# Other step orders in a two-layer hybrid network: the recurrence, the attention, half-array products without mutual order, and the last tile's low part in a bank of its own

## The chip, the cores and the metric

The kernel runs on one core of one Trainium2 chip. The metric is the device time of one execution in microseconds (us), lower being better. The engines are TensorE (PE in the profile, its weight loads PEld), VectorE (DVE), ScalarE (ACT), GpSimd (POOL) and SyncE (SP), which here issues nearly all transfers.

## The reference, cut to what matters

Two layers run over 256 tokens of width 1024. Layer 0 mixes tokens by a gated linear recurrence (HGRN2, 8 heads of 128), layer 1 by sparse attention (NSA, 16 query heads, 4 key heads, three branches: compressed, selected and windowed). A SwiGLU network of hidden width 2816 follows each mixer.

```
for layer in range(2):
    h = modulate(x, norm_mix[layer], shift, scale)
    y = hgrn2_mixer(h, ...) if layer == 0 else nsa_mixer(h, ..., nsa_shared_kv(...))
    x = x + gate * y
    h = modulate(x, norm_ffn[layer], shift, scale)
    x = x + gate * ((silu(h @ w_a) * (h @ w_b)) @ w_out)
```

Shift, scale and gate come from a vector c by one matrix for each sublayer (the ada products). All is float32.

## The kernel before

**Precision.** Each weight tile is split into a high part wh (ScalarE casts it to f32r, L321) and a low part wl (VectorE subtracts, L325); activations are split likewise. A product is the sum of three f32r products, wh by high, wh by low, wl by high (mm3, L531 to L533; tok_steps, L983 to L985, with the operands' roles exchanged), each over 128x128 weights and 256 columns. Where high and low activations lie side by side, the first two are one product of 512 columns (gemm_wide, L543), and wl by high is one of 256 (L544). Products of 32 or 64 weight columns (level_scores, ada_pe, head_norm, attend_values) are in plain fp32; they use a part of the array's columns, four or two of them side by side.

**Order of the work.** A weight tile of 1 MB is loaded by SyncE in the order of SCHED through a ring of 4, cast and split when its turn comes (process, fetch). ORDER["hgrn"] and ORDER["nsa"] are lists written by hand; they set in which order the program's steps are written, and SCHED follows from them. The framework's scheduler then lists the instructions of each engine by priority (PRI, high_priority) and by the dependencies known to it; an engine takes its list in order.

**The recurrence (hgrn).** In its list D builds the decays of a pair of head pairs, i and g are weight products (values hg_i, gates hg_g), S the scores of a pair (hgrn_scores: psl for levels 0 to 4 and psu for level 5, in the 32-column form, psx for the last level), V the products of scores and values (hgrn_values: hgpv, L1134 to L1136, fp32 on the whole array, waiting for the masked scores A), T the normalised values' transposes (values_end: hgt), o the output product (hgo). A step with + is not written at its place: it is a generator put into the row `between`, and hgrn_scores takes steps from it, 4 after each of its 12 blocks of a level in S0/4 and S1/4. The token x writes whatever is left.

**The attention (nsa).** In its list c is half of the compression (cmp), q a query product (nq0 to nq3, its copies huq and hsqq and the rotation usq, QR on ScalarE and VectorE), K the normalised input for keys and values, G the gates product, n the norm of two queries (hs, hb), w a product for values (tiles v0 and v1 of the profile), x the compressed branch (cs, its softmax css on VectorE and ScalarE, its transpose pct), s the scores of one pair of heads (L1521, maxima mx and exponentials Pt, normalised at L1547), v the values of one pair (transposes ptt at L1561, copies PT at L1564 and L1566, products po at L1578) and a one tile of the ada products (L427: adapsg, adapsss, with the transpose adat). attend_values is listed late (offset 10 of "av"), rotate early (offset -15 of "rot").

**The end.** In the second SwiGLU network each of the eight output tiles of 128 columns is 22 steps of gemm_wide into the two halves of one PSUM bank, and residual (L796) adds first the low half, then the high half, to x; for the last network it then writes the tile to memory (L800).

## Time and profile before

| what | value |
|---|---|
| median of 3 runs (lowest, highest) | 726.69 us (726.45, 727.84) |
| the profiled execution | 726.5 us |
| its span | 724.7 us |
| TensorE busy | 711.4 us, 98% |
| VectorE busy | 578.6 us, 80% |
| ScalarE busy | 433.7 us, 60% |
| recurrence, first psl to first hgo product | 70.7 to 146.7 us |
| attention, first hs to first nso product | 384.3 to 508.5 us |

The profile is of one execution, taken by the hardware. The span is what its records cover; 1.8 us of the execution's time lie around it. A row of the timeline has the start in us, the duration, the engine, the line and the operation with output and inputs; "x4" counts records, and an fp32 product has two. A duration of TensorE includes the pipeline's run, so what one product takes of its time is read from start to start. The view of waits names the engine and line that waited and what it waited for, with the sum, the times and the longest in us.

### The profile page before, as it was taken

How to read it: one execution, taken by the hardware profiler on the slowest of the kernel's cores; microseconds unless marked ns; L12 is line 12 of the kernel's file. 1: busy time of each engine (PE TensorE's matmuls, PEld its weight loads, DVE VectorE, ACT ScalarE, POOL GpSimd, SP SyncE). 2: the span in 40 equal slices, each digit the busy share in tenths (PEclk: the TensorE clock that was granted, in tenths of full speed). 3: DMA queues.
4: the chain of work that ended last, by engine and by line, in shares of the span. 5: the costliest groups of instructions: out<-in, count | busy, mean ns of one | idle time of the engine just before them, and what ended most of it. 6: DMA issues, size and time to landing. Idle time of an engine off the chain costs nothing.

```text
span 724.7 us, 14519 instructions
## 1 busy us (share of the span) xinstructions
PE 711.4 (98%) x5821; PEld 626.3 (86%) x5821; DVE 578.6 (80%) x1177; ACT 433.7 (60%) x849; POOL 0.4 (0%) x5
## 2 busy tenths in 40 slices
PE   7999999999999999999998999999999999999997
PEld 4998788799999999988897996555999888888886
DVE  6997896589999889889598898677779878776651
ACT  5669877567635454544379776558657656564430
POOL 0000000000000000000000000000000000000000
PEclk9999999999999999999999999999999999999999
DMA  8899865734599889889546631663745757556710
GB/s 354 323 395 359 338 249 187 282 117 175 176 335 378 318 334 345 317 307 339 194 147 232 232 124 52 233 233 123 284 175 175 250 207 256 205 196 231 256 65 23
DMA packets 27158, 172.48 MB, mean 238 GB/s; under 512 B 2897, under 2 KB 4305, under 8 KB 7250
## 3 DMA queue, kind: packets, MB, share of 16 engines
q1 hardware_dynamic: 26656, 170.80, 64.2%
q8 instruction: 46, 0.75, 0.4%
q10 hardware_dynamic: 434, 0.74, 0.3%
q14 instruction: 22, 0.18, 0.1%
HBM read 170.48 MB, written 1.05 MB: 237 GB/s over the span
## 4 chain that ended last, share of the span: by engine, by line
PE 84%; ACT 7%; DVE 6%; DMA 2%; issue 1%; ACTq 0%
PE ffo L543 11%; PE ff L531 6%; PE ff L533 6%; PE ff L532 6%; PE ffo L544 6%; PE ff L543 5%; PE po L1578 3%; PE ff L544 2%; PE adapsss L427 2%; PE ptt L1561 2%; PE s L1521 1%; PE nso L531 1%; ACT wh L321 1%; PE nso L533 1%; PE cmp L1416 1%; PE hg_g L531 1%
## 5 line engine op out<-in xcount | busy, mean ns | idle before, releaser
L321 ACT CAST wh<-raw 128x1024 fp32r<-128x1024 f32 x199 | 206.7, 1048 | 152.2 <-PE ffo L543 47.7
L325 DVE TENSOR_TENSOR wl<-raw,wh 128x1024 fp32r<-128x1024 f32 x199 | 241.3, 1222 | 64.7 <-ACT wh L321 64.4
L543 PE MATMUL ffo<-g,wh 128*128 128x512 f32 x352 | 123.6, 394 | 0.0
L532 PE MATMUL ff<-hl,wh 128*128 128x256 f32 (+1 forms) x352 | 99.2, 282 | 0.0
L544 PE MATMUL ffo<-g,wl 128*128 128x256 f32 x352 | 99.1, 282 | 0.0
L533 PE MATMUL ff<-hh,wl 128*128 128x256 f32 (+1 forms) x352 | 99.1, 282 | 0.0
L531 PE MATMUL ff<-hh,wh 128*128 128x256 f32 (+1 forms) x352 | 99.0, 282 | 0.0
L543 PEld LDWEIGHTS ffo<-g,wh 128*128 128x128 f32 x352 | 66.2, 188 | 15.5
L389 DVE CUSTOM_DVE_ANT_0 junk<-raw,crep 128x1024 f32<-128x1024 f32 x64 | 78.0, 1218 | 0.5 <-DMA raw<-in_w 0.4
L531 PEld LDWEIGHTS ff<-hh,wh 128*128 128x128 f32 x352 | 66.3, 189 | 0.2 <-ACT hh L582 0.2
L533 PEld LDWEIGHTS ff<-hh,wl 128*128 128x128 f32 x352 | 66.5, 189 | 0.0
L532 PEld LDWEIGHTS ff<-hl,wh 128*128 128x128 f32 x352 | 66.4, 189 | 0.0
L544 PEld LDWEIGHTS ffo<-g,wl 128*128 128x128 f32 x352 | 66.1, 188 | 0.0
L543 PE MATMUL ff<-h,wh 128*128 128x512 f32 x152 | 54.1, 394 | 0.0
L544 PE MATMUL ff<-h,wl 128*128 128x256 f32 x152 | 42.6, 281 | 0.0
L543 PEld LDWEIGHTS ff<-h,wh 128*128 128x128 f32 x152 | 28.7, 189 | 6.6
L465 ACT ACTIVATE Pt<-Pt,nm 128x128 f32<-128x128 f32 x64 | 28.2, 443 | 8.5 <-DVE nm L1530 8.4
L796 DVE SCALAR_TENSOR_TENSOR x<-ffo,mod,x 128x256 f32<-128x256 f32 x32 | 15.4, 482 | 20.0 <-PE ffo L544 19.7
L544 PEld LDWEIGHTS ff<-h,wl 128*128 128x128 f32 x152 | 28.7, 189 | 0.0
L526 ACT CAST g<-fg 128x256 fp32r<-128x256 f32 x44 | 17.8, 404 | 17.8 <-DVE fg L1201 16.7
L1526 DVE CUSTOM_DVE_ANT_0 Pt<-s,cst 128x128 f32<-128x128 f32 (+1 forms) x64 | 19.1, 352 | 2.8 <-PE s L1521 2.8
L1037 DVE TENSOR_TENSOR rf<-rf 128x512 f32<-128x512 f32 x28 | 18.5, 692 | 2.2 <-ACT X L1034 1.2
(490 smaller groups left out, 1733.2 us busy)
## 6 DMA issues: line engine op xcount, KB each, us to landing
raw<-in_w SPq DMA_DIRECT2D x153, 1024.0 KB, 5.1
raw<-in_w SPq DMA_DIRECT2D x11, 512.0 KB, 6.6
w1late<-in_w SPq DMA_DIRECT2D x2, 1024.0 KB, 6.1
x<-in_x SPq DMA_DIRECT2D x2, 512.0 KB, 4.9
out<-x SPq DMA_DIRECT2D x8, 128.0 KB, 1.9
cst<-in_cst ACTq DMA_DIRECT2D x1, 558.0 KB
rselr<-in_rsel SPq DMA_DIRECT2D x1, 256.0 KB, 3.7
w<-in_w SPq DMA_DIRECT2D x1, 128.0 KB, 3.6
```

What stands on the lines that cost most here:

```text
L321: r = nc.scalar.copy(wh, u)
L325: r = nc.vector.tensor_tensor(wl, u, wh.bitcast(F32), op=ALU.subtract)
L389: r = nc.vector.tensor_tensor_reduce(out=junk, in0=t[:, h * D:(h + 1) * D], in1=self.crep, scale=1.0, scalar=0.0, op0=ALU.mult, op1=ALU.ad ...
L465: r = nc.scalar.activation(out, in_, func, **kw)
L531: mm(ps, lhsT=wh, rhs=hh, start=first, stop=False)
L532: mm(ps, lhsT=wh, rhs=hl, start=False, stop=False)
L533: return mm(ps, lhsT=wl, rhs=hh, start=False, stop=last)
L543: mm(ps, lhsT=w[k][0], rhs=b, start=k == 0, stop=False)
L544: mm(ps[:, 0], lhsT=w[k][1], rhs=b[:, 0], start=False, stop=k == n - 1)
L1037: nc.vector.tensor_tensor(fr, fr, ap(rf, 2 * W, [1, 2], [2, n], [0, b]), op=ALU.mult)
L1526: nc.vector.tensor_tensor_reduce(out=Pt[half][:, br, o:o + n], in0=ps[half][:, br], in1=cs[:, S - n:], scale=1.0, scalar=-3e38, op0=ALU.ad ...
L1578: nc.tensor.matmul(po[64 * half:64 * half + 64, t], lhsT=w[:, half], rhs=rhs, start=n == 0, stop=n == len(steps) - 1, tile_position=(0, 64 ...
```

## The change

There are four edits.

1. ada_pe (L427) and attend_values (L1578) declare no dependency between products that write other partitions of the same PSUM tile. No instruction is added; the scheduler may list them in another order.
2. In the recurrence, V0 moves behind D1, i2 and i3's place, and +g3 behind S1/4. S1 has 48 places for steps; i3 (16), g2 (16) and T0 (2) fill 34 of them, and g3 is written unbroken by x.
3. In the attention the compression and the gates come before nq0, nq2 before the values' products and the first norm, nq3 after both values' products, and the ada steps earlier among the last pairs. SCHED, and with it the order of the weight tiles, follows.
4. The last output tile puts its 22 low products into a bank of its own (ffo1_low), adds them to x, and then takes 44 products of 256 columns (wh and wl by the high part) into the other bank, whose one residual step is followed by the output.

The assert writes no instruction. The diff:

```diff
 
 ORDER = {
     "hgrn": (
-        "D0 k i0 +g0 +i1 +g1 S0/4 x c0 c1 V0 D1 i2 +i3 +g2 +T0 +g3 S1/4 x G0 V1 T1 o0 H o1 G1 o2 o3"
+        "D0 k i0 +g0 +i1 +g1 S0/4 x c0 c1 D1 i2 +i3 V0 +g2 +T0 S1/4 +g3 x G0 V1 T1 o0 H o1 G1 o2 o3"
     ).split(),
     "hada": [1, 1, 2, 2, 3, 3, 4, 4, 7, 7, 8, 8],
     "f0": [7, 7, 8, 8, 9, 13, 15, 16, 16, 16, 21, 21, 22, 23, 25, 26, 28, 29, 31, 32],
     "nsa": (
-        "q0 c1 c0 K G q1 n0 x0 w0 s0 q3 s1 q2 w1 s2 v0 v1 n1 s3 a s4 v2 a v3 a x1 s5 a a s6 v4 v6 s7 v5 a v7 a a a a a a"
+        "c1 c0 G q0 K q1 q2 n0 x0 w0 s0 s1 w1 q3 s2 v0 v1 n1 s3 a s4 v2 a v3 a a x1 s5 a s6 a v4 v6 s7 a a v5 a v7 a a a"
     ).split(),
     "f1": [15, 16, 24, 29],
 }
@@ -423,10 +423,13 @@
         ks = [i] if ss else [2 * i, 2 * i + 1]
         last = i == (7 if ss else 3)
         for n, k in enumerate(ks):
+            row = []
             for j in range(4):
-                nc.tensor.matmul(self.aps[32 * j:32 * j + 32, :q], lhsT=self.c32[:, k],
-                                 rhs=t[:, n * D + j * q:n * D + (j + 1) * q], start=k == 0, stop=k == KD - 1,
-                                 tile_position=(0, 32 * j))
+                row.append(nc.tensor.matmul(self.aps[32 * j:32 * j + 32, :q], lhsT=self.c32[:, k],
+                                            rhs=t[:, n * D + j * q:n * D + (j + 1) * q], start=k == 0, stop=k == KD - 1,
+                                            tile_position=(0, 32 * j)))
+                for r in row[:-1]:
+                    self.tc.declare_no_dep(row[-1].ins, r.ins, query=mybir.DependencyQuery.ANY, reason="other partitions")
         if not last:
             return
         m, A, bias = self.ada_tiles(l)
@@ -965,6 +968,7 @@
                 elif t[0] == "o":
                     for _ in out_steps(n):
                         pass
+            assert next(between, None) is None
             self.end_residual(nxt)
             self.h = nxt
 
@@ -1216,8 +1220,19 @@
                             tiles[nch * 16 + 8 * h + e] = t
                     nch += 1
                 ps = self.acc_tile(f"ffo{l}_{m}")
-                self.gemm_wide(ps, [tiles.pop(m * NF + k) for k in range(NF)], lambda k: g[:, k])
-                self.residual(ps[:, 0], m, gate, nxt, ps[:, 1])
+                ws = [tiles.pop(m * NF + k) for k in range(NF)]
+                if nxt is None and m == KD - 1:
+                    mm, pl = nc.tensor.matmul, self.acc_tile(f"ffo{l}_low")
+                    for k in range(NF):
+                        mm(pl[:, 0], lhsT=ws[k][0], rhs=gl[:, k], start=k == 0, stop=k == NF - 1)
+                    self.residual(pl[:, 0], m, gate, nxt, part=True)
+                    for k in range(NF):
+                        for e in range(2):
+                            mm(ps[:, 0], lhsT=ws[k][e], rhs=gh[:, k], start=k == 0 and not e, stop=k == NF - 1 and e == 1)
+                    self.residual(ps[:, 0], m, gate, nxt)
+                else:
+                    self.gemm_wide(ps, ws, lambda k: g[:, k])
+                    self.residual(ps[:, 0], m, gate, nxt, ps[:, 1])
             self.end_residual(nxt)
             self.h = nxt
 
@@ -1572,11 +1587,16 @@
             for e, t in ((0, slice(0, S)), (1, slice(P, S))):
                 steps.append((br, self.V[:, e, br, P * g:P * g + P].rearrange("p (h d) -> p h d", h=2),
                               slice(0, S) if e == 0 else slice(S, 384), t))
+        done = [], []
         for n, (br, w, r, t) in enumerate(steps):
             for half in range(2):
                 rhs = r if br is None else PT[half, br][:, r]
-                nc.tensor.matmul(po[64 * half:64 * half + 64, t], lhsT=w[:, half], rhs=rhs, start=n == 0,
-                                 stop=n == len(steps) - 1, tile_position=(0, 64 * half))
+                done[half].append(nc.tensor.matmul(po[64 * half:64 * half + 64, t], lhsT=w[:, half], rhs=rhs, start=n == 0,
+                                                   stop=n == len(steps) - 1, tile_position=(0, 64 * half)))
+        for a in done[0]:
+            for b in done[1]:
+                self.tc.declare_no_dep(b.ins, a.ins, query=mybir.DependencyQuery.ANY, reason="other partitions")
+                self.tc.declare_no_dep(a.ins, b.ins, query=mybir.DependencyQuery.ANY, reason="other partitions")
         self.split(self.O[0][:, j, :256], self.O[1][:, j, :256], po)
```

On TensorE, where the first values' products (hgpv) stand in the recurrence; in the names the last number counts buffers, hg_i2 is a values' product of f32r, hgpv0 and hgpv1 are those of the first two head pairs. Before:

```order
L1134 MATMUL hgpv0_1388<-v0_755,A0_1366 128x128
L1135 MATMUL hgpv0_1388<-v0_755,A0_1366 128x128
L1136 MATMUL hgpv0_1388<-v0_755,A0_1366 128x128
L983 MATMUL hg_i2_1493<-wh28_0_1245,h0_181 128x256
L984 MATMUL hg_i2_1493<-wl28_0_1246,h0_181 128x256
L1134 MATMUL hgpv1_1400<-v0_755,A1_1379 128x128
L1135 MATMUL hgpv1_1400<-v0_755,A1_1379 128x128
L1136 MATMUL hgpv1_1400<-v0_755,A1_1379 128x128
```

After:

```order
L988 MATMUL hg_i2_1460<-wl28_1_1250,h0_181 128x256
L989 MATMUL hg_i2_1460<-wh28_1_1249,h0_181 128x256
L1138 MATMUL hgpv0_1521<-v0_755,A0_1366 128x128
L1139 MATMUL hgpv0_1521<-v0_755,A0_1366 128x128
L1140 MATMUL hgpv0_1521<-v0_755,A0_1366 128x128
L1138 MATMUL hgpv0_1521<-v0_755,A0_1366 128x128
L1139 MATMUL hgpv0_1521<-v0_755,A0_1366 128x128
L1140 MATMUL hgpv0_1521<-v0_755,A0_1366 128x128
L1138 MATMUL hgpv1_1533<-v0_755,A1_1379 128x128
```

Before, hg_i2 is broken into by hgpv0 and by hgpv1; now all 48 of its products stand ahead of both.

On TensorE, at the end of the second scores; psu2 and psu3 are of the 32-column form, hg_g3 is a gates product of f32r. Before:

```order
L532 MATMUL hg_g3_1883<-h0_181,wh33_1_1712 128x256
L533 MATMUL hg_g3_1883<-h0_181,wl33_1_1713 128x256
L1114 MATMUL psu3_1919<-s1_758 32x64 x2
L1118 MATMUL psu3_1919<-X3_5_1483 32x32 x2
L1114 MATMUL psu3_1919<-s1_758 32x64 x2
L1118 MATMUL psu3_1919<-X3_5_1483 32x32 x2
L1114 MATMUL psu3_1919<-s1_758 32x64 x2
L1118 MATMUL psu3_1919<-X3_5_1483 32x32 x2
L1114 MATMUL psu3_1919<-s1_758 32x64 x2
L1118 MATMUL psu3_1919<-X3_5_1483 32x32 x2
L531 MATMUL hg_g3_1883<-h0_181,wh33_1_1712 128x256
```

After:

```order
L1122 MATMUL psu2_1864<-X2_5_1446 32x32 x2
L1118 MATMUL psu3_1865<-s1_758 32x64 x2
L1122 MATMUL psu3_1865<-X3_5_1450 32x32 x2
L1118 MATMUL psu3_1865<-s1_758 32x64 x2
L1122 MATMUL psu3_1865<-X3_5_1450 32x32 x2
L1118 MATMUL psu3_1865<-s1_758 32x64 x2
L1122 MATMUL psu3_1865<-X3_5_1450 32x32 x2
L1118 MATMUL psu3_1865<-s1_758 32x64 x2
L1122 MATMUL psu3_1865<-X3_5_1450 32x32 x2
L428 MATMUL adapsss1_1097<-raw34_1580,c32_103 32x512 x3
L428 MATMUL adapsss1_1097<-raw35_1699,c32_103 32x512 x4
L534 MATMUL hg_g3_1964<-h0_181,wh33_0_1708 128x256
```

Before, psu2 and psu3 each stand between products of hg_g3; now psu3 follows psu2, ada products of the same form follow, and hg_g3 comes behind them.

On ScalarE, in the attention, after the last exponentials of pair 1 (Pt1): V copies a values' product, huq3, hsqq3 and usq3 belong to query product nq3, hry is the norm's first step, PT0 are copies of pair 0's transposes, Pt2 the exponentials of pair 2. Before:

```order
L465 ACTIVATE Pt1_5585,sm_5584<-Pt1_5585,nm_5602 128x256
L1339 COPY V_4660<-v1_5690 128x2x256
L465 ACTIVATE hry_5867<-hs_5862,eps_88 128x256
L1566 COPY PT0_10_5793<-ptt_5794 128x384
L1566 COPY PT0_01_5799<-ptt_5800 128x384
L465 ACTIVATE Pt2_5752,sm_5751<-Pt2_5752,nm_5769 128x128
```

After:

```order
L468 ACTIVATE Pt1_5585,sm_5584<-Pt1_5585,nm_5602 128x256
L1243 COPY huq3_5738<-nq3_5689 128x512
L1245 ACTIVATE hsqq3_5740<-nq3_5689 128x512
L1255 COPY usq3_5742<-huq3_5738 32x512 x4
L468 ACTIVATE hry_5867<-hs_5862,eps_88 128x256
L1581 COPY PT0_10_5793<-ptt_5794 128x384
L1581 COPY PT0_01_5799<-ptt_5800 128x384
L468 ACTIVATE Pt2_5752,sm_5751<-Pt2_5752,nm_5769 128x128
```

Where one copy of v1 stood between the exponentials of pair 1 and hry, there stand now the three steps on nq3.

## The prediction

> **What bounds the kernel now.** I read the page first: busy shares, slices, granted clock, the chain.
>
> ```profile
> span 724.7 us, 14519 instructions
> PE 711.4 (98%) x5821; PEld 626.3 (86%) x5821; DVE 578.6 (80%) x1177; ACT 433.7 (60%) x849; POOL 0.4 (0%) x5
> PE   7999999999999999999998999999999999999997
> PEclk9999999999999999999999999999999999999999
> PE 84%; ACT 7%; DVE 6%; DMA 2%; issue 1%; ACTq 0%
> L796 DVE SCALAR_TENSOR_TENSOR x<-ffo,mod,x 128x256 f32<-128x256 f32 x32 | 15.4, 482 | 20.0 <-PE ffo L544 19.7
> ```
>
> TensorE is busy 98% of the span at full clock in every slice, and 84% of the chain that ended last is its work. So time goes only if TensorE does less, stands still less, or if something leaves the few us after its last product. The change leaves the amount of arithmetic as it was. What remains are three things: waits of TensorE, the price of changing the form in which its array is used, and the tail. The waits of TensorE come second:
>
> ```profile
> PE hs L1255 <- ACT hsqk L1305: 1.0, 1, 1.0
> PE nq L531 <- ACT wh L321: 1.0, 1, 1.0
> PE s L1521 <- DVE mx L1526: 0.7, 2, 0.4
> ```
>
> All three lie in the attention stage, 2.7 us together. No wait of the recurrence is in this view at such a size; what is to be won there are changes of form.
>
> **The recurrence.** The timeline of TensorE shows one visit of the 32-column form (psl, fp32) between full-array f32r products (hg_i, L983 to L985):
>
> ```profile
> 117.89 0.27 PE L985 MATMUL hg_i<-wh,h 128*128 128x256 f32 x1
> 118.10 0.45 PE L1108 MATMUL psl<-X 128*32 128x16 f32 x32
> 118.47 0.39 PE L983 MATMUL hg_i<-wh,h 128*128 128x256 f32 x1
> 118.70 0.28 PE L984 MATMUL hg_i<-wl,h 128*128 128x256 f32 x1
> 118.82 0.28 PE L985 MATMUL hg_i<-wh,h 128*128 128x256 f32 x1
> ```
>
> Start to start an f32r product of 256 columns takes 0.12 us (118.70 to 118.82). Into psl it takes 0.21, so entering costs 0.09. The first f32r product after it takes 0.23, 0.11 too much; I add 0.09 for leaving the form, an estimate set equal to the entry. Coming back is thus 0.20, a round trip 0.29. Between f32r and fp32 products that both use the whole array it is cheaper:
>
> ```profile
> 103.80 0.28 PE L985 MATMUL hg_i<-wh,h 128*128 128x256 f32 x1
> 104.15 0.49 PE L1135 MATMUL hgpv<-v,A 128*128 128x128 f32 x2
> 105.14 0.39 PE L1136 MATMUL hgpv<-v,A 128*128 128x128 f32 x2
> 105.29 0.37 PE L983 MATMUL hg_i<-wh,h 128*128 128x256 f32 x1
> 105.49 0.28 PE L984 MATMUL hg_i<-wl,h 128*128 128x256 f32 x1
> ```
>
> The first product after hgpv takes 0.20 (105.29 to 105.49), 0.08 too much, and the way in some 0.07: 0.15 a round trip. From 103.80 to 104.15 there are 0.35 us where 0.12 and 0.07 are due: a wait of 0.16 for the masks A.
>
> I count the changes of form in the listed order between the first psl and the first hgo product: 65 before, 54 after. Of these, f32r to 32 columns go from 23 to 19 (4 x 0.09 = 0.36), the way back from 24 to 21 (3 x 0.20 = 0.60), f32r to whole-array fp32 and back from 14 to 9 (2.5 x 0.15 = 0.38), and one change between fp32 forms is added (0.09). That is -1.25. The wait for A goes too, since 48 products of hg_i2 (5.7 us) now stand ahead of hgpv: -0.15. Sum -1.4.
>
> What it may cost: the values' normalisation chain starts about 5 us later against the score blocks. hgt0 and hgt1 need o0 and o1, and in the new order only six f32r products stand between the last adaps product and adat, which needs ScalarE's copy. Before, hgt1's place already shows a short wait:
>
> ```profile
> 130.80 1.90 PE L427 MATMUL adapsss<-raw,c 128*32 128x512 f32 x10
> 132.78 0.65 PE L1163 MATMUL hgt<-cst,o 128*128 128x128 f32 x4
> ```
>
> In the 1.98 us up to the second hgt stand a group of four column products and one torn from the next group; at the 1.06 us that a group's row has they fill it, without its pipelined end (some 0.9 each) 0.2 is a wait. If two such waits are added and the changes of form are worth only their cheap 0.07 each, the recurrence brings 11 x 0.07 - 0.4 = 0.4; if each is worth the dear 0.20 and no wait comes, 11 x 0.20 + 0.15 = 2.3. I take 1.4, since each part has its own row.
>
> **No ordering between half-array products.** TensorE takes its list in order, so the edit acts only through the list. Halves side by side run together; a torn pair does not:
>
> ```profile
> 449.67 1.08 PE L1578 MATMUL po<-PC,VC 128*64 128x256 f32 x4
> 454.39 1.30 PE L1578 MATMUL po<-PT,V 128*64 128x256 f32 x10
> ```
>
> Four records of one half (two products) need 1.08 us; ten of paired halves 1.30. An unpaired product of 256 columns is thus worth about 0.45. In the new list po's products form as many short groups as before and need one 256-column slot less (-0.45); hs, a column-tiled product without the edit, is torn once more (+0.45). Net 0, bounds -0.9 and +0.9.
>
> **The attention order.** By the same count, entries into f32r go from 18 to 15 (3 x 0.20), exits from 17 to 14 (3 x 0.09), changes between fp32 forms from 49 to 51 (2 x 0.09): -0.7. The waits of s for mx fall where VectorE put a rotation between the row maxima:
>
> ```profile
> 439.63 0.75 DVE L1244 SCALAR_TENSOR_TENSOR usq<-usq,cols,cst 128x512 f32<-128x512 f32 x1
> ```
>
> Now nq2's rotation is finished before s0: I take -0.5 of the 0.7. The other two waits of 1.0 (hs for hsqk, nq for a weight cast) keep their producers and nearly the queue ahead of these, so I leave them; they are worth 1.0 each if they went.
>
> Against this stand two new waits. First, pct follows the softmax chain of the compressed branch:
>
> ```profile
> 429.35 1.42 PE L1485 MATMUL cs<-KC,QN 128*128 128x32 f32 x12
> 436.15 0.42 DVE L1501 TENSOR_TENSOR css<-css,cmx 128x256 f32<-128x256 f32 x1
> 436.86 0.38 PE L1504 MATMUL pct<-cst,css 128*128 128x128 f32 x2
> ```
>
> The chain ran from 430.8 to 436.6, 5.8 us, with three rotation steps of about 0.7 on VectorE among its own, and TensorE filled the gap with 52 f32r products. Now 35 stand there, 35 x 0.12 = 4.2 us. If all three rotation steps are gone from it the chain takes 3.7 and nothing waits; if none is, 1.6 us are waited. I take a chain of 4.7, halfway, as subtractions of weights may stand in their place: +0.5.
>
> Second, nq3 takes v1's place as the filler between the scores of pairs 1 and 2 (21 products, 2.5 us, instead of 39, 4.6 us), and it is followed on ScalarE by three steps, not one. ScalarE's rows there:
>
> ```profile
> 436.48 0.60 ACT L1230 ACTIVATE hsqq<-nq 128x512 f32<-128x512 f32 x1
> 437.09 2.50 ACT L1240 COPY usq<-huq 32x512 f32<-32x512 f32 x4
> 441.39 0.40 ACT L465 ACTIVATE Pt<-Pt,nm 128x128 f32<-128x128 f32 x1 [1.80 <-DVE nm L1530]
> 448.43 0.58 ACT L1339 COPY V<-v 128x512 f32<-128x512 f32 x1
> 451.39 0.47 ACT L465 ACTIVATE hry<-hs,eps 128x256 f32<-128x256 f32 x1 [2.38 <-PE hs L1255]
> ```
>
> After the exponentials (441.39 to 448.4) came one copy of 0.58 and 2.38 of idle time, 2.96. Now huq, hsqq and usq of nq3 stand there: 0.6 + 0.6 + 2.5 = 3.7. Behind them are queued hry and the copies PT of the transposed probabilities, and behind those the exponentials of pair 2, on which ptt waits. So ScalarE delivers 0.7 us later while TensorE, with 18 fillers less, asks 2.1 us earlier: 2.8 less slack. How much there was is bounded by the idle 2.38 and by the ada products (adapsg) that stand ahead of the later ptt; I take +0.7, with 0 and +2.8 as ends. Sum of the attention: -0.7 - 0.5 + 0.5 + 0.7 = 0.0; ends -1.2 and +3.2.
>
> **The tail.** The last tile's timeline:
>
> ```profile
> 720.19 0.28 PE L544 MATMUL ffo<-g,wl 128*128 128x256 f32 x1
> 720.31 0.39 PE L543 MATMUL ffo<-g,wh 128*128 128x512 f32 x1
> 720.32 0.19 PEld L544 LDWEIGHTS ffo<-g,wl 128*128 128x128 f32 x1
> 720.54 0.28 PE L544 MATMUL ffo<-g,wl 128*128 128x256 f32 x1
> 720.86 1.00 DVE L796 SCALAR_TENSOR_TENSOR x<-ffo,mod,x 128x256 f32<-128x256 f32 x2 [6.67 <-PE ffo L544]
> 721.89 0.33 SPq L800 DMA_DIRECT2D out<-x  x1
> ```
>
> A wide pair takes 0.35 (720.19 to 720.54), 22 pairs 7.7 us; three products of 256 columns at 0.12 take 0.36, as much. Two residual steps (L796, 482 ns each) stood behind the last product; one is now done under the 44 products of the high part. -0.5, because nothing else stands between product and output.
>
> The new split has 22 weight loads more, one for each 256 columns instead of one for 512. The page counts as many loads as products (PEld and PE, 5821 each), so hg_i's products above have one each, and follow at 0.12 us all the same. [...]
>
> **Sum.** -1.4 (recurrence) + 0 (halves) + 0.0 (attention) - 0.5 (tail) = -1.9. The profiled execution took 726.5, 724.7 of it span and 1.8 around it; the median of the runs is 726.69. So 726.69 - 1.9 = 724.8.
>
> **The rivals.** *A, the attention order gives the gain back* (0.17). ScalarE's longer queue costs 2.0 instead of 0.7 and pct 0.8: the attention is at +1.6, the sum at -0.3, 726.4. For it: 2.8 us of slack are taken; against it: 2.38 of idle time were there.
>
> *B, slower* (0.11). The one mechanism is ScalarE's queue between pair 1 and pair 2: when hry and PT come late, pair 2's exponentials and, one after the other, the pairs behind it come late, so that the wait is paid at two pairs. It decides from 4.1 us at this place on (0.7 and the 3.4 up to 728.14); with 4.2 the time is 728.3. For it: each pair's 3.5 us of exponentials (16 of them from 441.39 to 448.4 for two pairs) stand in one queue. Against it: the ada products moved between the pairs are there to fill.
>
> *C, the attention gains as well* (0.14): neither new wait shows and one of the two waits of 1.0 goes with the moved weights: -1.2 - 1.0 in the attention, 722.6.
>
> *D, weight loads show in the tail* (0.03): were each of the 22 new loads to stand between two products with its profiled 0.19, the tail would be 4.2 longer and the time 729.0. [...] The stream of hg_i, with a load for each product, speaks against it.
>
> *That the change does nothing* can't be for the tail; for the freed halves it is my forecast.
>
> **How the numbers follow.** The forecast holds 0.55, with its own range of 723.6 to 726.0. A measurement of this kernel tells about 0.2% from no change, 1.45 us: faster is below 725.24, slower above 728.14. Of the 0.55 I count 0.40 as faster, 0.15 as same; C adds 0.14 to faster, A 0.17 to same, B 0.11 and D 0.03 to slower: 0.54, 0.32, 0.14. The range of 722.6 to 727.5 takes in A and C and leaves B out.
>
> **What would show it.** The stretch from the first psl product to the first hgo product should be about 1.4 us shorter, with hgpv unbroken behind hg_i2 and psu2, psu3 in one piece. The wait of s for mx should be gone; new rows should name pct behind css, and ptt or po behind ScalarE's PT. At the end one L796-like step of 0.5 us should stand between the last product and the output. The prediction is wrong if the recurrence gains under 0.5, if TensorE waits over 3 us more in the attention, or if the last tile's products take over 8.5 us.

## The result and the profile after

The changed kernel took 722.24 us (median of 6 runs, 721.75 to 723.39), the kernel before beside it 726.57 (6 runs, 726.22 to 727.84): a ratio of 0.9939, 95% interval 0.9926 to 0.9952, which is 4.4 us less (3.5 to 5.4). The forecast was 1.9 less, and 724.8 with a range down to 722.6: the sign was right, the size under half, and the time lies just outside the range. The profiled execution took 721.75. From the page of the changed kernel, the span, the busy shares, the granted clock's slices, and the chain's shares:

```profile
span 720.0 us, 14569 instructions
PE 708.3 (98%) x5843; PEld 626.2 (87%) x5843; DVE 579.6 (80%) x1177; ACT 433.4 (60%) x849; POOL 0.4 (0%) x5
PEclk9999999999999999999999999999999999999999
PE 88%; ACT 6%; DVE 4%; issue 1%; DMA 1%; SPq 0%; ACTq 0%
```

TensorE is still the bound, at full clock (98% busy, a mean granted clock of 1.00); the other engines have the same work. To find where the time went I cut each span at five starts on TensorE: the first psl, hgo, hs, the second network's first ff, and the last product. Those of the changed kernel, by its timeline:

```profile
69.81 0.55 PE L1112 MATMUL psl<-q,X 128*32 128x48 f32 x32
144.20 0.36 PE L534 MATMUL hgo<-oh,wh 128*128 128x256 f32 x1
381.67 0.62 PE L1270 MATMUL hs<-hsqk,cst 128*32 128x256 f32 x4
526.38 0.28 PE L534 MATMUL ff<-hh,wh 128*128 128x258 f32 x1
716.30 0.28 PE L1231 MATMUL ffo<-g,wl 128*128 128x256 f32 x1
```

With the same starts of the trace of before (70.65, 146.71, 384.26, 530.68, 720.54):

| stretch | before | after | difference | forecast |
|---|---|---|---|---|
| start to first psl | 70.65 | 69.81 | -0.84 | none |
| recurrence, to first hgo | 76.06 | 74.39 | -1.67 | -1.4 |
| rest of layer 0, to first hs | 237.55 | 237.47 | -0.08 | 0 |
| attention, to first ff | 146.42 | 144.71 | -1.71 | 0.0 |
| second network, to the last product | 189.86 | 189.92 | +0.06 | 0 |
| behind the last product | 4.16 | 3.70 | -0.46 | -0.5 |
| span | 724.7 | 720.0 | -4.70 | -1.9 |

The first row isn't the change's: two kernels below whose first 70 us are those of before reach psl at 69.96 (the attention's order alone) and 70.44 (the tail alone). Without it the change is worth 3.9 us, inside the measured interval. The second row has a scatter too: the profiled executions with the old list of the recurrence take 75.88 to 76.41 for it, those with the new one 74.39 to 74.90, 1.5 less by their medians. The attention is the term that was missed. The windows of these two stretches give the length, TensorE's busy time and the granted clock, before and after:

```profile
384.26:530.68 146.42, 143.31 (x1101) 1.00 0.52 193
```

```profile
381.67:526.38 144.71, 142.00 (x1102) 1.00 0.51 190
```

TensorE is busy 1.31 us less and stands still 0.40 less (3.11 to 2.71). At an equal clock I put that down to the list: fewer changes of form, or fewer torn groups (products on different columns of the array run side by side as a group: in a run below eight records of one take 1.07 us, and two alone 1.05; a group is torn when other products stand between its members). And the waits, forecast to grow by 0.7, have shrunk. The view of waits of the changed kernel, the rows of the attention:

```profile
PE nq L534 <- ACT wh L321: 0.8, 1, 0.8
PE po L1594 <- DVE mx L1541: 0.7, 1, 0.7
PE adat L441 <- ACT adasm L438: 0.5, 1, 0.5
PE hs L1270 <- ACT hsqk L1320: 0.5, 1, 0.5
PE ptt L1576 <- DVE Pt L1562: 0.2, 1, 0.2
```

The row of s behind mx is gone, as forecast. pct and the copies PT, for which 0.5 and 0.7 were put in, have no row. po waits, but for VectorE's maxima; adat's wait is new; and hs waits half as long as before.

### The profile page after: what moved, and what is told of

Its sections match the earlier page's. It is cut to its first block, busy times and chain, and to the rows that moved or that the text cites. A ratio compares the mean times of both kernels' runs of the same rounds, so it can differ in the third digit from the quotient of the medians.

```text
span 720.0 us, 14569 instructions
## 1 busy us (share of the span) xinstructions
PE 708.3 (98%) x5843; PEld 626.2 (87%) x5843; DVE 579.6 (80%) x1177; ACT 433.4 (60%) x849; POOL 0.4 (0%) x5
## 3 DMA queue, kind: packets, MB, share of 16 engines
HBM read 170.48 MB, written 1.05 MB: 238 GB/s over the span
## 4 chain that ended last, share of the span: by engine, by line
PE 88%; ACT 6%; DVE 4%; issue 1%; DMA 1%; SPq 0%; ACTq 0%
PE ffo L546 11%; PE ff L534 7%; PE ff L536 7%; PE ff L535 6%; PE ffo L547 5%; PE ff L546 5%; PE po L1594 2%; PE ff L547 2%; PE adapsss L428 2%; PE ptt L1576 2%; PE s L1536 2%; PE hg_g L534 1%; PE nso L534 1%; PE hgo L534 1%; PE hg_g L536 1%; PE nso L536 1%
## 5 line engine op out<-in xcount | busy, mean ns | idle before, releaser
L546 PE MATMUL ffo<-g,wh 128*128 128x512 f32 x330 | 116.0, 394 | 0.0
L547 PE MATMUL ffo<-g,wl 128*128 128x256 f32 x330 | 93.0, 282 | 0.0
L546 PEld LDWEIGHTS ffo<-g,wh 128*128 128x128 f32 x330 | 62.0, 188 | 14.5
L547 PEld LDWEIGHTS ffo<-g,wl 128*128 128x128 f32 x330 | 61.9, 188 | 0.0
```

The costliest lines, as they stand in the source:

```text
L546: mm(ps, lhsT=w[k][0], rhs=b, start=k == 0, stop=False)
L547: mm(ps[:, 0], lhsT=w[k][1], rhs=b[:, 0], start=False, stop=k == n - 1)
```

## The experiments

The theories at the start: each edit brings its own term, the prediction's account with the attention's term mis-sized; or the attention's gain is that of the freed halves, which let the scheduler keep groups of column products whole; or a part of the tail is lost to weight loads. The first four runs do one part of the change each, on the kernel before.

**The recurrence's order alone.**

```diff
-        "... c0 c1 V0 D1 i2 +i3 +g2 +T0 +g3 S1/4 x G0 ..."
+        "... c0 c1 D1 i2 +i3 V0 +g2 +T0 S1/4 +g3 x G0 ..."
```

> The kernel before with the new step order of the recurrence alone. Theory P (the parts add, each paying in its own stretch): the stretch from the first psl to the first hgo product shrinks from 76.05 to about 74.4 us, nothing else changes, time -1.7 us (725.0 beside 726.6). Rival Q (the stretches help each other: an earlier recurrence shifts the loads and with them the waits of the attention): less than -1.0 here, with the rest appearing only together with the attention order.

724.40 us, a ratio of 0.9977 (0.9964 to 0.9990): 1.7 us less. Its stretch from psl to hgo is 74.69, 1.37 less than before, and its attention is unchanged (146.32).

**The attention's order alone.**

```diff
-        "q0 c1 c0 K G q1 n0 x0 w0 s0 q3 s1 q2 w1 s2 v0 v1 n1 s3 a s4 v2 a v3 a x1 s5 a a s6 v4 v6 s7 v5 a v7 a a a a a a"
+        "c1 c0 G q0 K q1 q2 n0 x0 w0 s0 s1 w1 q3 s2 v0 v1 n1 s3 a s4 v2 a v3 a a x1 s5 a s6 a v4 v6 s7 a a v5 a v7 a a a"
```

> The kernel before with the new step order of the attention alone, no freed halves. Theory P: the stretch from the first hs product to the second network's first product shrinks by 1.4 to 1.8 us of the 1.72 seen with all edits, time about -1.6 (725.0). Rival F (the freed halves make the gain of the attention): within 0.5 us of the kernel before.

724.75 us, 0.9980 (0.9971 to 0.9989): 1.45 less. The window of its attention:

```profile
383.46:528.51 145.05, 142.68 (x1102) 1.00 0.51 189
```

1.37 less than before: 0.63 of busy time, and 0.74 of standing still (3.11 to 2.37). So the order alone gains, and more than half of it is waits.

**The tail alone.**

```diff
-                self.gemm_wide(ps, [tiles.pop(m * NF + k) for k in range(NF)], lambda k: g[:, k])
-                self.residual(ps[:, 0], m, gate, nxt, ps[:, 1])
+                ws = [tiles.pop(m * NF + k) for k in range(NF)]
+                if nxt is None and m == KD - 1:
...
+                    self.residual(pl[:, 0], m, gate, nxt, part=True)
...
+                    self.residual(ps[:, 0], m, gate, nxt)
```

> The kernel before with the last tile's low part in its own bank alone. Theory P: the 66 products of the last tile take as long as the 44 before (7.7 us), one residual step of 0.48 us goes from behind the last product: -0.5 to -0.7 us (726.0). [...]

726.25 us, 0.9997 (0.9987 to 1.0008): too little for these runs to tell. The trace shows it. The end of this kernel's timeline:

```profile
720.76 0.28 PE L1227 MATMUL ffo<-g,wl 128*128 128x256 f32 x1
721.08 0.48 DVE L796 SCALAR_TENSOR_TENSOR x<-ffo,mod,x 128x256 f32<-128x256 f32 x1 [4.70 <-PE ffo L1227]
```

From the last product to the span's end (724.4) it is 3.64, 0.52 less than before, with one residual step of 0.48 where there were two. That the new loads add time is refuted. In the chain of waits of the changed kernel the last tile's two runs of products are

```profile
708.81 2.59 PE ffo_low L1227 x22
711.40 5.20 PE ffo L1231 x44
```

66 products in 7.79 us, 0.118 each, with as many loads of 0.19 us, whose starts are 0.12 apart as well. Rival D of the prediction put 4.2 us more.

**The freed halves alone.**

```diff
+                for r in row[:-1]:
+                    self.tc.declare_no_dep(row[-1].ins, r.ins, query=mybir.DependencyQuery.ANY, reason="other partitions")
...
+        for a in done[0]:
+            for b in done[1]:
+                self.tc.declare_no_dep(b.ins, a.ins, query=mybir.DependencyQuery.ANY, reason="other partitions")
+                self.tc.declare_no_dep(a.ins, b.ins, query=mybir.DependencyQuery.ANY, reason="other partitions")
```

> The kernel before with only the dependencies between half-array products taken away. Theory P: the list changes at a few places among the ada and po products, 0 within 0.4 us. Rival F (the freed halves make the gain of the attention): -1.2 to -1.7 us, and po's products stand in unbroken pairs.

726.41 us, 0.9996 (0.9987 to 1.0004), which the runs can't tell from none. The attention of the trace is 0.61 shorter, where two unchanged attentions (in the first and the third run) repeat that of before within 0.10:

```profile
383.31:529.12 145.81, 142.71 (x1101) 1.00 0.52 194
```

Busy time falls by 0.60, standing still not at all (3.10). By line, one kind of product falls clearly, and po's products rise by some 0.3. Of the attention's adapsss products, which stand four columns side by side, these are the groups (64 records; busy us, mean ns) of before, of this run, of the order alone, and of the whole change:

```profile
L427 PE MATMUL adapsss<-raw,c 128*32 128x512 f32 x64 | 10.0, 601 | 0.0
```

```profile
L428 PE MATMUL adapsss<-raw,c 128*32 128x512 f32 x64 | 9.1, 603 | 0.0
```

```profile
L427 PE MATMUL adapsss<-raw,c 128*32 128x512 f32 x64 | 11.0, 603 | 0.0
```

```profile
L428 PE MATMUL adapsss<-raw,c 128*32 128x512 f32 x64 | 10.2, 603 | 0.0
```

The same 64 records take 0.8 to 0.9 less wherever the columns are freed, with the old order (10.0 to 9.1) and with the new one (11.0 to 10.2): about what one group of four takes (in the kernel before, two such groups in a row, sixteen records, take 1.92 us, and one 1.07). I read this as one torn group less.

The two parts add up to -1.98 in the attention, the whole has -1.71. With the recurrence (-1.37) and the tail (-0.52) the four parts come to -3.9 in their traces, as the whole does without its start. The next runs ask which piece of the order gives the gain: three pieces on the kernel before.

**Compression and gates first.**

```diff
-        "q0 c1 c0 K G q1 n0 x0 ..."
+        "c1 c0 G q0 K q1 n0 x0 ..."
```

> The kernel before with only the head of the attention's list new: compression and gates ahead of the first query product. Theory C (the wait of hs for hsqk was made by a weight cast of 1.05 us that stood between ScalarE's steps, and the new head puts this cast ahead): the wait of 1.16 us at hs falls to about 0.2, the stretch from first hs to the second network's first product goes from 146.4 to about 145.4 us, time -1.0 (725.2). Rival (the wait moves on to the next product that waits for a cast): wait at hs gone, stretch unchanged within 0.3.

728.68 us, 1.0038 (1.0026 to 1.0050). The forecast of 725.2 is missed by 3.5 us with the wrong sign, although the wait of hs for hsqk, on which it rests, did halve (0.5, from 1.0). The attention is 148.30 long, 144.85 of it busy: 1.54 more busy time than before, and 0.34 more of standing still. By line, po's products take 2.5 more and ptt's 1.3 more, adapsss 1.5 less.

**nq2 early, nq3 late.**

```diff
-        "... n0 x0 w0 s0 q3 s1 q2 w1 s2 v0 ..."
+        "... q2 n0 x0 w0 s0 s1 w1 q3 s2 v0 ..."
```

> The kernel before with only the middle of the attention's list new: nq2 before the values' products, the last query product as the last filler. Theory W (the rotation of nq2 between the row maxima costs 0.8, and the shorter filler costs new waits of ptt and po of about 0.9): stretch within 0.5 us of 146.4, no gap of 1.0 among the first scores, time 726.4. Rival (the new waits belong to the new head of the list): stretch 145.4, time -1.0.

726.23 us, 1.0001 (0.9993 to 1.0010), as forecast: nothing. Its trace shows two sides: s no longer waits for mx (0.7 before), but po now waits 0.7 behind VectorE's mx and ptt 0.3 behind ScalarE's hsqq, so there the feared queue behind nq3 does show.

**The ada steps earlier.**

```diff
-        "... v2 a v3 a x1 s5 a a s6 v4 v6 s7 v5 a v7 a a a a a a"
+        "... v2 a v3 a a x1 s5 a s6 a v4 v6 s7 a a v5 a v7 a a a"
```

> The kernel before with only the end of the attention's list new: the ada steps earlier among the last pairs. Theory S (the gain among the scores of pairs 3 and 4 of some 1 us comes from other work standing between them): stretch -0.5 to -1.0, time 725.9. Rival (that gain comes from the queries that are finished earlier): stretch unchanged within 0.2, time 726.5.

729.49 us, 1.0048 (1.0036 to 1.0060); 725.9 was forecast. In its trace the attention stands still as before (3.12) and is busy 4.84 longer: adapsss 2.1 and po 2.2, and a drop of the clock of the kind described at the end. So two pieces lose 2.4 and 3.2 us, one does nothing, and all three together win 1.4. The pieces of such a list don't add, and a forecast for a piece by its own waits is worth little.

**Only nq3 and the second values' product exchanged, in the changed kernel.** By the prediction's ScalarE queue this takes the queue away.

```diff
-        "... s0 s1 w1 q3 s2 v0 ..."
+        "... s0 s1 q3 w1 s2 v0 ..."
```

> The changed kernel with the last two fillers exchanged back: the query product nq3 before the values' product v1. Theory D (po waits 0.65 and ptt 0.2 because VectorE has the normalisation of pair 0, 1.8 us, ahead of the maxima that free the banks, and 21 products are too short a cover): with v1's products as the cover both waits go, the stretch is 143.9 instead of 144.7, time -0.8 against the changed kernel (721.5). Rival A (ScalarE's queue decides, as the prediction had it): ScalarE gets nq3's three steps earlier and pair 2's exponentials start about 0.7 sooner after those of pair 1; the gain is the same, but po's wait would be named after ScalarE in the changed kernel and pair 3 would gain too.

731.86 us, 1.0080 (1.0067 to 1.0092), 9.6 more than the changed kernel where 0.8 less was forecast. The window of its attention:

```profile
382.93:537.45 154.52, 151.82 (x1101) 1.00 0.48 178
```

It is 9.81 longer than after, all of it busy (+9.82); it stands still 2.70, as after. po's wait is gone, as the first theory had it, and ptt's has grown to 0.8, so that the sum is unchanged: no wait did this. The adapsss group and a piece of the timeline of TensorE in this run:

```profile
L428 PE MATMUL adapsss<-raw,c 128*32 128x512 f32 x64 | 14.3, 603 | 0.0
```

```profile
494.05 1.07 PE L428 MATMUL adapsss<-raw,c 128*32 128x512 f32 x8
495.06 0.64 PE L1593 MATMUL po<-PC,VC 128*64 128x256 f32 x2
...
496.13 1.05 PE L428 MATMUL adapsss<-raw,c 128*32 128x512 f32 x2
497.11 0.65 PE L1593 MATMUL po<-PC,VC 128*64 128x256 f32 x2
497.68 1.06 PE L428 MATMUL adapsss<-raw,c 128*32 128x512 f32 x6
```

Eight records (four column products, side by side) take 1.07 us; a torn group takes 1.05 for its first two records and 1.06 for the other six. Read from start to start it is the same: 1.01 for the eight, 0.98 for the two. A tear thus costs a whole group. adapsss alone has 4.1 us more busy time than after, po 3.9, s 1.6, hs 1.2 and ptt 1.0 (they overlap in part). One exchange of two names in the list moved all this: the scheduler's list, not the waits, set the time here.

This suggested a new theory: the count of torn groups and changes of form sets the attention's time. If so, groups that can't be torn should win.

**Unbreakable groups.** In three runs the four ada products stand in a critical section of the framework: in the kernel of the last run, in the changed kernel, and there together with the pairs of hs, s and po.

```diff
+            with self.tc.tile_critical() if l in (2, 3) else ExitStack():
                 for j in range(4):
                     nc.tensor.matmul(...)
```

> The kernel of e8 (changed kernel with nq3 ahead of v1) whose four column products of each ada step in the attention are one unbreakable group of the list. Theory T (torn groups and changes of form set the time of this stage): against e8 the list has the second ada product's groups down from 14 to 8 (6 x 0.86), the gate's from 9 to 8 (0.43), the norm's from 7 to 5 (2 x 0.43) and 106 changes of form down to 80 (26 x 0.12): -9.5 us, 722.4. Rival W (the longer time of e8 comes from waits behind VectorE and ScalarE): it stays above 728.

> The changed kernel with the same unbreakable ada groups in the attention. Theory T: ada groups from 10 to 8 and from 9 to 8 (2 x 0.86 + 0.43), changes of form from 80 to 75 (0.6), the norm's groups 5 to 4 (-0.43), one pair of po and one of s torn more (+0.9): -2.2 us against the changed kernel, 720.0. Rival W: the ada products were cover for waits, unbroken they leave these open: within 0.7 us of the changed kernel (722.2).

> The changed kernel with all products that share the array in the attention in unbreakable groups: ada, the norm's, the scores' and po's halves. Theory T: beyond e10 the po groups fall from 48 to 40 (3.9), the scores' from 18 to 16 (1.3), the norm's rise by one (0.43), changes of form from 75 to 83 (1.0): -3.8 against e10 before new waits, some 1.0 of them: 717.5. Rival W: halves of po that wait for each other cost more than they save: not under e10.

769.96 us (1.0602, 1.0587 to 1.0616), 762.03 (1.0492, 1.0477 to 1.0506) and 900.22 (1.2388, 1.2371 to 1.2405). The theory fails in all three. Two of the rival's bounds hold (above 728, not under the second run), but not for its reason, so the runs tell nothing of torn groups: a section also makes TensorE wait at its start (1.24 to 1.38 us at four groups). One group of the changed kernel with whole ada groups, by the timeline:

```profile
459.56 1.08 PE L428 MATMUL adapsg<-raw,c 128*32 128x256 f32 x8 [1.24 <-PEq L426]
```

The group is whole, and TensorE stands idle 1.24 us ahead of it behind its own sequencer (PEq); at the next three groups it is 1.34, 1.27 and 1.38. That run also waits twice over 5 us for a weight tile (DMA), and its clock in the attention is 0.89.

**Only +g3 moved, on the kernel before.** This asks which of the recurrence's two moves it is.

```diff
-        "... +g2 +T0 +g3 S1/4 x ..."
+        "... +g2 +T0 S1/4 +g3 x ..."
```

> The kernel before with only +g3 moved behind the second scores, V0 left at its place. Theory P (each change of form has its price): of the 11 changes saved in the recurrence most belong to g3, the stretch from first psl to first hgo shrinks by 0.8 to 1.0 of the 1.4 to 1.7, time -0.9 (725.6). Rival (the wait for the masks A and the visits of hgpv are the larger part): less than -0.5.

726.01 us, 0.9992 (0.9981 to 1.0003). From psl to hgo it is 75.00 (70.16 to 145.16), 1.06 less than before, as forecast. The run of the whole recurrence has 0.3 more, less than the scatter of this stretch, so that V0's part isn't shown; its move alone wasn't tried. By the median the kernel gains only 0.1, which is the rival's number, with an interval of -1.4 to +0.2 that holds the forecast's -0.9 too. A possible reason, not shown: 5 of its 11 executions, the profiled one among them, have a mean granted clock of 0.997, against 2 of 15 at 0.997 or 0.998 of the kernel before beside it. In the profiled one the clock falls in the attention, where nothing was changed (below).

**Torn on purpose, in the changed kernel.** The columns 2 to 4 of each ada group are held until the first is issued, so that they fall apart.

```diff
+                with ExitStack() as near:
+                    if j and l in (2, 3):
+                        near.enter_context(self.tc.issue_after(row[0].ins))
+                        near.enter_context(self.tc.high_priority())
                     row.append(nc.tensor.matmul(...))
```

> The changed kernel in which the last three column products of each ada step in the attention may only follow the first and are listed later, so that other products come between; no work and no synchronisation between engines is added. Theory T (torn groups and changes of form set the time): second ada product's groups from 10 to 17 (7 x 0.86), the gate's from 9 to 16 (7 x 0.43), po's from 47 to 56 (9 x 0.4), changes of form from 80 to 108 (28 x 0.12): about +16 us against the changed kernel, 738. Rival W (waits behind VectorE and ScalarE set it, and torn products fill them): under +5, 727.

737.86 us, 1.0157 (1.0139 to 1.0174); 738 was forecast from the list's count. Its attention:

```profile
382.00:542.53 160.53, 157.23 (x1102) 1.00 0.45 171
```

15.8 longer than after, 15.2 of it busy time: adapsss has 5.3 more, adapsg 3.0 and po 5.2. Tears, with the changes of form that come with them, cost 15 us here.

**Whole by priority, in the kernel with nq3 and the values exchanged.** The ada groups get a higher priority, which keeps them whole without a section.

```diff
+            with self.tc.high_priority(offset=400) if l in (2, 3) else ExitStack():
+                row = []
```

> The kernel of e8 (731.9) with the ada steps of the attention given a higher priority, so that each group of four stands whole in the list; no branch, no new work. Theory T: ada groups from 14 to 8 (-5.2) and from 9 to 8 (-0.4), the norm's from 7 to 4 (-1.3), po's from 50 to 52 (+0.6), changes of form from 106 to 99 (-0.8): about -7 us, 725. Rival W: the waits of e8 stay, within 2 us of 731.9.

733.46 us, 1.0102 (1.0082 to 1.0122): the rival's number, not the theory's. The window, the adapsss group and the largest waits:

```profile
383.84:541.15 157.31, 149.74 (x1101) 0.98 0.47 175
```

```profile
L429 PE MATMUL adapsss<-raw,c 128*32 128x512 f32 x64 | 7.9, 600 | 0.0
```

```profile
PE ptt L1576 <- DVE Pt L1562: 1.9, 1, 1.9
PE ptt L1576 <- ACT PT L1581: 1.6, 1, 1.6
```

The tears of adapsss are gone (7.9, from 14.3 in the run it builds on), and TensorE stands still 7.57 us, 4.87 more. The ada products, now early and in one piece, no longer fill the waits for the softmax. The clock takes a part as well (0.98 in this window; 0.50 from 484 to 488 and 0.68 from 488 to 492), so that busy time falls by only 2.08. The profiled execution (736.61) is the slowest of the six.

**The list chosen by count alone.** Of many orders of the last part I took the one with the fewest torn groups and changes of form.

```diff
-        "... v0 v1 n1 s3 a s4 v2 a v3 a a x1 s5 a s6 a v4 v6 s7 a a v5 a v7 a a a"
+        "... v0 v1 s3 n1 v2 a a v3 s4 a a x1 s5 a s6 v6 a v4 a a s7 v5 a v7 a a a"
```

> The changed kernel with another attention list, chosen by the count of torn groups and changes of form alone: ... v0 v1 s3 n1 v2 a a v3 s4 a a x1 s5 a s6 v6 a v4 a a s7 v5 a v7 a a a. Theory T: second ada product's groups from 10 to 9 (-0.86), po's from 47 to 45 (about even in length), the norm's from 5 to 4 (-0.43), the scores' from 17 to 18 (+0.4), changes of form from 80 to 74 (-0.7): -1.5 us against the changed kernel, 720.7. Rival W: the order has never been tried against the waits, they grow by as much or more: 722 or over.

735.54 us, 1.0129 (1.0108 to 1.0150), 13.3 more than the changed kernel; 720.7 was forecast. The window of its attention and its largest waits there:

```profile
381.88:539.40 157.52, 145.85 (x1101) 0.97 0.47 174
```

```profile
PE ptt L1575 <- DVE Pt L1561: 2.8, 3, 2.3
PE adapsss L428 <- DMA raw<-in_w: 2.3, 1, 2.3
PE adat L441 <- ACT adasm L438: 2.1, 1, 2.1
```

TensorE stands still 11.67 us, 9.0 more than after. Its busy time is 3.85 longer, but the granted clock explains more than that: it drops three times there, and one such drop costs 1.5 us in another run (both at the end), which makes 4.4. At full clock the busy time would have been some 0.6 shorter (an estimate from these runs), on the side that the count said (1.5 shorter). The theory of the count may have the sign of its own term right and fails as a whole. No run beat the changed kernel.

## Why the prediction was wrong in size

**What bounds the kernel: right.** TensorE remains the bound (98% busy) at full clock (1.00), and only its list, its waits and the tail changed.

**The recurrence: right.** -1.4 forecast; -1.67 with the whole change and -1.37 alone, -1.5 by the medians of all profiled executions. hgpv stands unbroken behind hg_i2, and the wait for its masks is gone; the changed kernel's timeline:

```profile
107.67 0.28 PE L989 MATMUL hg_i<-wh,h 128*128 128x256 f32 x1
107.79 0.38 PE L1138 MATMUL hgpv<-v,A 128*128 128x128 f32 x2
```

0.12 from the last hg_i product to hgpv, where 0.35 stood. Neither of the two feared waits appears; the move of +g3 is the larger part (1.06). The prediction saw no wait of the size of 0.7 in this stretch. There is one of 0.6, of hg_g for a weight's low part from VectorE, but it stands in both kernels, so nothing hangs on it.

**The tail: right.** -0.5 forecast, -0.46 and -0.52 measured. Forecast 7.7 us for its products, measured 7.79. 66 loads of 0.19 us each lie under the 66 whole-array products here, which follow each other at 0.118 us all the same; the 4.2 us that rival D put for the 22 new loads did not appear.

**The attention: wrong.** The step that failed is "Sum of the attention: -0.7 - 0.5 + 0.5 + 0.7 = 0.0", with the halves' "Net 0" beside it. Measured is -1.71, beyond the sum's lower end of -1.2: 1.1 of the miss lies in TensorE's waits (+0.7 forecast, -0.40 measured), 0.6 in its busy time (-0.7 forecast, -1.31 measured). By its terms:

- Changes of form, -0.7: the order alone has 0.63 less busy time, but that doesn't show the term. Busy time holds tears as well: adapsss has 1.0 more there and hs 1.0, po<-PC 1.5 less. The agreement is of the sum, and may be luck.
- The waits, +0.7 together (-0.5 + 0.5 + 0.7): wrong by sign. The order alone has -0.74 of standing still, the whole change -0.40. s for mx gives 0.7, a little more than forecast. pct, for which +0.5 was put in, has no wait, since its chain was taken too long. VectorE before, then VectorE and TensorE of the changed kernel:

```profile
432.14 1.22 DVE L325 TENSOR_TENSOR wl<-raw,wh 128x1024 fp32r<-128x1024 f32 x1
...
434.07 0.42 DVE L1516 TENSOR_TENSOR css<-css,cmx 128x256 f32<-128x256 f32 x1
434.55 0.44 PE L1519 MATMUL pct<-cst,css 128*128 128x128 f32 x2
```

The chain, which starts at 430.40, takes 4.1 us, not 4.7, and the fillers' 4.2 cover it. Two of the three rotation steps are still in it. Gone from it are the third (0.74) and a weight subtraction of 1.22 us, which the prediction hadn't counted in the old chain.

- The queue behind nq3, +0.7. It was real on ScalarE, but nobody waited for it there. TensorE, VectorE and ScalarE at that place, changed kernel:

```profile
445.07 1.29 PE L1594 MATMUL po<-PC,VC 128*64 128x256 f32 x8 [0.65 <-DVE mx L1541]
...
442.46 1.83 DVE L1562 TENSOR_TENSOR Pt<-Pt,cf 128x768 f32<-128x768 f32 x2
444.21 0.28 DVE L1541 CUSTOM_DVE_ANT_0 Pt<-s,cst 128x128 f32<-128x128 f32 x1
...
445.33 0.56 ACT L1243 COPY huq<-nq 128x512 f32<-128x512 f32 x1
```

po starts at 445.07, before the first of the three nq3 steps on ScalarE (445.33). It is VectorE's normalisation (1.83 us at 442.46) that stands ahead of the maxima for which po waits: 0.65. That this is about the number forecast is luck, since it comes from another engine.

- The waits that were left out: "keep their producers and nearly the queue ahead of these, so I leave them". The queue ahead of hsqk did change. ScalarE before:

```profile
386.00 1.05 ACT L321 CAST wh<-raw 128x1024 fp32r<-128x1024 f32 x1
386.95 0.50 ACT L1305 ACTIVATE hsqk<-u,sw 128x256 f32<-128x256 f32 x1
```

and after:

```profile
379.84 1.06 ACT L321 CAST wh<-raw 128x1024 fp32r<-128x1024 f32 x1
...
382.20 0.51 ACT L1320 ACTIVATE hsqk<-u,sw 128x256 f32<-128x256 f32 x1
...
384.44 0.51 ACT L1320 ACTIVATE hsqk<-u,sw 128x256 f32<-128x256 f32 x1
...
382.76 0.62 PE L1270 MATMUL hs<-hsqk,cst 128*32 128x256 f32 x2 [0.46 <-ACT hsqk L1320]
```

A weight cast of 1.05 us stood right ahead of the last hsqk, for which TensorE waited 0.99. In the new order the last cast stands 4.6 us ahead of it, and nobody waits for it; the 0.46 that is left is a wait for the hsqk before it, at 382.20. nq's wait for its cast fell by 0.2 as well. The order of ScalarE's instructions would have shown it. (The run with compression and gates first halved the wait of hs in the same way.)

- The freed halves, 0: -0.60 alone and -0.68 of busy time beside the new order (142.68 to 142.00), where half is lost again to standing still (2.37 to 2.71; adat's wait of 0.5, which neither part has alone, is new). I counted po and hs and not the four columns of ada_pe, which the same edit frees and of which one group fewer is torn.

**The rivals.** A and B, the ScalarE queue giving the gain back, didn't come about. C, "the attention gains as well", gives 722.6 and is nearest: one of its two waits fell by half, and neither feared wait showed where it was put. Its price is near by its sum only, since 0.6 of the gain is the freed halves'. D is refuted. None of the prediction's own signs of being wrong came about: all of them were signs of a smaller gain, none of a larger one.

One sentence of the kernel's description is the wrong way round: a positive offset lists earlier, as the run with an offset of 400 shows, whose last adapsss product starts at 475.6 where it was 515.0. So attend_values with its 10 is listed early, and rotate with -15 late. No step of the prediction rests on it.

**What stays open.** Shown is that the attention's -1.71 is -1.31 of TensorE's busy time and -0.40 of standing still, and that each of the two can move by 9 us or more by itself. Which single move of the list brings it isn't settled: the pieces don't add, and the scheduler's list changes as a whole. The changed kernel without the freed halves is only known as the sum of three runs (724.40, 724.75 and 726.25).

## What to carry to other kernels

Where a scheduler makes the list, count torn groups and changes of form for every product that an edit touches (here the ada columns, not only po), and read for each wait which instruction now stands right ahead of its producer, on every engine. Then weigh both together: whole groups shorten TensorE's list (adapsss from 14.3 to 7.9 us here) but can leave the waits unfilled (standing still from 2.70 to 7.57). Here a list chosen for the count alone lost 13 us, and making the groups whole in a list that had lost 9.6 won nothing back. Try the whole order, since its pieces say little of it.

## What the runs showed of the hardware

- In the run with nq3 and the values exchanged, a group of column products costs as much for 2 of its records as for 8 (1.05 and 1.07 us), so a tear costs a whole group.
- The granted clock below 1 is a mean. By windows of 1 us, in the run with the counted list it is 0.50 from 484 to 486, from 498 to 500 and from 515 to 517, with a part of the us on either side, each time behind a wait of TensorE (2.28, 2.15 and 2.05 us), and 1.00 around. Each drop lasts some 3.5 us (an estimate: the stretch from 474 to 494, at 0.91, loses 1.8 us of clock in one drop, and that from 494 to 519, at 0.86, 3.5 in two, each at half clock). One us of the second drop:

```profile
498.00:499.00 1.00, 1.00 (x6) 0.50 0.95 401
```

  In the run with only +g3 moved there is one such drop in the profiled execution (0.50 from 441 to 444), while TensorE was busy all the time. The last wait before it is 0.43 us, and the kernel before has such a wait there too, without a drop in its profiled execution. So the length of a wait doesn't explain it alone, and what does stays open. The drop costs 1.5 us (that attention is 147.90 long, 146.42 before).
- Ahead of four groups in critical sections of the framework TensorE stood idle 1.2 to 1.4 us behind its own sequencer; at the other groups the trace names other waits.
- The start up to the first psl, which no edit here touches, took between 69.8 and 71.4 us in sixteen profiled executions, so a span's difference under 1 us is read by stretches.
